# A two-layer decoder trunk on one core: attention's projections one step later, two of them held back, and longer delays in two chains

## The chip, the core and the metric

The kernel runs on one core of one Trainium2 chip, as one launch. The time is the device time of that core in microseconds. Every time below is from runs of the unchanged kernel or from the one execution that the profiler recorded.

## What is computed

Two layers on 256 tokens of width 1024, in fp32; layer 0 mixes tokens by a gated MLP, layer 1 by native sparse attention (NSA). Each layer also attends to 256 memory tokens, projects both results together, and ends with a SwiGLU feed-forward part.

```python
for i in range(2):
    h = rmsnorm(x, norm_mix[i])
    mem_n = rmsnorm(mem, norm_mem[i])
    mix, mem_q = gmlp_mixer(h, ...) if i == 0 else nsa_mixer(h, ...)
    mem_o = mem_cross_attention(mem_q, mem_n, w_mem_kv[i])    # 4 heads of 64
    x = x + concat([mix, mem_o]) @ w_out                      # 1024 -> 1024
    h = rmsnorm(x, norm_ffn[i])
    x = x + (silu(h @ wg) * (h @ wu)) @ wd                    # 1024 -> 2816 -> 1024
return rmsnorm(x, norm_final)
# gmlp_mixer: u, v = split(gelu(h @ w_in)); v = rmsnorm(v) * gain
#   mixed = per group g of 12: tril(w_s[g]) @ v[:, g] + b_s[g];  returns u * mixed
# nsa_mixer: 12 query heads, 4 key/value heads; compressed, selected and sliding
#   branches, each a softmax, summed with gates. k and v of the compressed branch:
#   silu(blocks @ w1) @ w2, 15 blocks of 32 tokens
```

## The kernel before

**Products.** Each fp32 operand is split into a high part H and a rest L, both fp32r, and each product is three matmuls into one PSUM bank: H by H, L by H, H by L (`mm3`, L228 to L230). `split` (L121) makes a pair: ACT copies the source to H (`wH`, `aH`, L122), then DVE subtracts H from the source (`wL`, `aL`, L123); `split_gained` (L127, L128) does it with a gain. So each weight tile of 128x1024 costs one ACT and one DVE pass, and waits for its DMA (`raw`, three buffers) and for one of seven slots for split weights; the slot comes free when the tile's last product has been made. Activations are split in the same way on their way from PSUM to SBUF. Two PSUM pools of four banks each are used: `mm` for sums that stay, `tr` for everything short-lived (transposes, scores, outputs of a head).

**Order.** The order of TensorE is the order in which the program is written (L90). Side chains (`v_chain`, `compress`, `mem_attention`, ...) are Python generators: `flow` keeps a running estimate of TensorE's time, adds to it at each product (`flow.tick`, L231), and resumes a chain when the time that it gave with `yield` is over. So `yield 3.0` says: put what follows on TensorE some 3 us of products later. ACT, DVE, POOL and the DMA queue are ordered by a scheduler, which takes the instruction of higher priority among those that are ready in its own plan; `tc.high_priority(offset=...)` lifts a stretch of code. `step` (L1015) runs its function with `HI = 150`. [...]

**Layer 0, the gate (L617 to L699).** `v_chain` transposes the masked w_s in three groups of four (L659, L660), ACT copies each to `wsT` (L661), `spatial(q)` makes four matmuls for each group (L639) and DVE adds the bias (L641); then four products `gm` of U and V (L671, DVE), each transposed (L674, line L244 of the helper) and split. Beside it TensorE does the projection of U (128x512 matmuls) and of the memory queries (128x256), whose result goes through L691 and L376 on DVE, and the memory keys and values (`mm<-mid,wH`).

**Layer 1, compression (L782 to L837).** The hidden layer of the compressed keys and values is summed in `ph` (L798), ACT applies Silu to its two halves (L808), and after a `yield` TensorE transposes it (L811, in the trace L244).

**Layer 1, attention (L1031 to L1072).** A step m of six handles one pair of heads. `scores(m)`: six matmul groups into four `tr` banks (L925, L927, L929); DVE adds the masks and finds the bounds (L945, L943); ACT takes the exponentials, eight of them (L949), and one for the compressed part (L961); DVE makes the scale `f` twice (L951, L952) and that of the compressed part, `smc` (L959 to L965); POOL multiplies the probabilities by `f` (L954), two passes each time. `turn(m)`: twelve transposes into three `tr` banks (L972, L978; L244), one more, `tc_`, into a fourth (L982), ACT copies them out (L974, L980, L983). `attend(m)`: 32 short matmuls into one `tr` bank `o` (L1001), then `split` (L1002): `aH` on ACT and `aL` on DVE. `mixed((m, tb))`: the output projection of that pair of heads for half tb of the tokens, six 128x512 matmuls (two `mm3`); it needs `aH` first and `aL` at its second matmul. The order at the end is

```python
step(scores, 4); mixed((0, 1)); step(attend, 2); step(turn, 3); mixed((2, 0))
step(scores, 5); mixed((1, 1)); step(attend, 3); step(turn, 4); mixed((3, 0))
step(attend, 4); step(turn, 5); mixed((4, 0), (2, 1)); step(attend, 5)
mixed((3, 1), (5, 0), (4, 1), (5, 1))
```

Of the kernel before, what the change touches and what calls it, by code (L numbers as in the profile page):

```python
# [26 lines left out]
class Flow:  # L27
# [10 lines left out]
    def _step(self):  # L38
        at, n, gen = heapq.heappop(self.heap)
        with self.tc.high_priority(offset=HI):  # L40
            try:
# [16 lines left out]


HI = 150  # L60
MEMLAT = 9.0
MEMCH = 0.0
VCH = 2.0
# [4 lines left out]
def body(tc, t, out):  # L68
    nc = tc.nc
    PE, ACT, DVE, POOL, SP = nc.tensor, nc.scalar, nc.vector, nc.gpsimd, nc.sync  # L70
    with ExitStack() as ctx:
# [49 lines left out]
        def split(H, L, src):  # L121
            ACT.copy(H, src)  # L122
            DVE.tensor_tensor(L, src, H.bitcast(F32), op=ALU.subtract)  # L123
# [118 lines left out]
        def transposes(ps, src, n, at=0):  # L242
            for j in range(n):
                PE.transpose(ps[:, (at + j) * 128 : (at + j + 1) * 128], src[:, j * 128 : (j + 1) * 128], ident)  # L244
            flow.now += n * 0.108

        def sumsq(src, acc, n):

            ACT.activation(junk[:, : src.shape[-1]], src, AF.Square, scale=n**-0.5, accum_out=acc)  # L249
# [17 lines left out]
        def blk(tb):  # L267
            return slice(tb * 128, (tb + 1) * 128)

        def kview(ps, n):  # L270
            return ps[:, : n * 128].rearrange("p (k n) -> p k n", k=n)
# [109 lines left out]
        def mem_attention(qTs, tb, kv, dst, done):  # L381
            qT = qTs[tb]

            scs = [tr(), tr()]
            for j in range(2):
                for i in range(2):
                    r = slice(i * 64, i * 64 + 64)
                    PE.matmul(scs[i][:, j * 256 : (j + 1) * 256], qT[r, j, :], kv[r, j, :], start=True, stop=True)  # L388
            flow.now += 1.1
            mx = tiny([128, 4], "mx")  # L390
            for i in range(2):
                DVE.reduce_max(mx[:, i * 2 : i * 2 + 2], scs[i].rearrange("p (j n) -> p j n", j=2), axis=AX.X)
            nb = tiny([128, 4], "nb")
            POOL.tensor_scalar(nb, mx, -SCALE, None, op0=ALU.mult)
            sm = tiny([128, 4], "sm")
            parts = [small([128, 2, 256]) for _ in range(2)]
            for i in range(2):
                for j in range(2):
                    n = i * 2 + j
                    ACT.activation(parts[i][:, j, :], scs[i][:, j * 256 : (j + 1) * 256], AF.Exp, bias=nb[:, n : n + 1],  # L400
                                   scale=SCALE, accum_out=sm[:, n : n + 1])
            rs = tiny([128, 4], "rs")
            DVE.reciprocal(rs, sm)
            for i in range(2):
                POOL.tensor_tensor(parts[i], parts[i], rs[:, i * 2 : i * 2 + 2].unsqueeze(2).to_broadcast([128, 2, 256]), op=ALU.mult)
            yield MEMLAT
            pTs = []
            for i in range(2):
                pt = tr()
                transposes(pt, parts[i].rearrange("p j n -> p (j n)"), 4)  # L410
                pT = small([128, 4, 128])
                ACT.copy(pT, kview(pt, 4))
                pTs.append(pT)
            yield 3.2
            o = tr()
            for j in range(2):
                for b in range(2):
                    for i in range(2):
                        h = (2 * j + i) * 64
                        PE.matmul(o[i * 64 : i * 64 + 64, blk(j)], kv[:, 2 + b, h : h + 64],  # L420
                                  pTs[i][:, j * 2 + b, :], start=b == 0, stop=b == 1)
            flow.now += 1.0
            split(dst[0][:, 6:8, blk(tb)], dst[1][:, 6:8, blk(tb)], kview(o, 2))
            done.append(1)
# [10 lines left out]
        def ffn(weights, nrm, after):  # L435
            accs = [[mm(), mm()], [mm(), mm()]]
            for ci, (nk, wg, wu, wd) in enumerate(weights):
# [4 lines left out]
                def gate(tb):  # L442
                    ps = tr()
                    gemm(ps, nrm.act, tb, wg, n)
                    sil[tb] = small([128, n])
                    with tc.high_priority(offset=HI):
                        ACT.activation(sil[tb], ps[:, :n], AF.Silu, scale=nrm.rstd[tb])
# [161 lines left out]
        def gelu(dst, ps, tb):  # L609
            with tc.high_priority(offset=HI):  # L610
                ACT.activation(dst, ps, AF.Gelu_apprx_tanh, scale=n0.rstd[tb])
# [36 lines left out]
        def v_chain():  # L648
            POOL.affine_select(wsr, wsr, pattern=[[0, 12], [-1, 128]], compare_op=ALU.is_ge, fill=0.0, base=0, channel_multiplier=1)
            for tb in range(2):  # L650
                ss = tiny([128, 2], "ss")
                sumsq(Vv[:, tb, 0:512], ss[:, 0:1], GW)
                sumsq(Vv[:, tb, 512:768], ss[:, 1:2], GW)
                r = rstd_of(ss)
                yield 1.5
                DVE.scalar_tensor_tensor(Vv[:, tb, :], Vv[:, tb, :], r, vg, op0=ALU.mult, op1=ALU.mult)
            yield 2.0
            for q in range(3):
                ps = tr()  # L659
                transposes(ps, wsr[:, q * 4 : q * 4 + 4, :].rearrange("p g s -> p (g s)"), 4)  # L660
                ACT.copy(wsT[:, q * 4 : q * 4 + 4, :], kview(ps, 4))  # L661
                yield 0.8
            for q in range(3):
                spatial(q)
                yield 1.0
            for c, n in ((0, 512), (512, 256)):
                for tb in range(2):
                    while tb not in u_done:
                        yield 0.3
                    gm = small([128, n])  # L670
                    DVE.tensor_tensor(gm, U[:, tb, c : c + n], Vv[:, tb, c : c + n], op=ALU.mult)  # L671
                    yield 1.0
                    ps = tr()
                    transposes(ps, gm, n // 128)  # L674
                    k = c // 128
                    split(mix[0][:, k : k + n // 128, blk(tb)], mix[1][:, k : k + n // 128, blk(tb)], kview(ps, n // 128))
            v_done.append(1)
# [8 lines left out]
        for tb in range(2):  # L686
            ps = mm()
            gemm(ps, n0.act, tb, WQ0, 256)
            mq = small([128, 256])
            with tc.high_priority(offset=HI):  # L690
                DVE.tensor_scalar(mq, ps[:, 0:256], n0.rstd[tb], None, op0=ALU.mult)  # L691
# [4 lines left out]
        for tb in range(2):  # L696
            flow.spawn(mem_attention(qT0, tb, kv0, mix, mo_done), 1.0 + 5.5 * tb)
# [34 lines left out]
        mix1 = acts()  # L732

        def rope(*a):
            with tc.high_priority(offset=HI):
                rope_(*a)
# [27 lines left out]
        def compress():  # L764
            X = [mqx[:, 512:1472].rearrange("p (a j n) -> p a j n", a=2, j=8),
                 mid([128, 2, 8, 60])]
            for s in range(2):
                for gp in range(2):
# [5 lines left out]
                    for part in range(2):  # L774
                        pe = gT[:, (PEV if s else PEK) + part * 8 : (PEV if s else PEK) + part * 8 + 8]
                        for par in range(2):
                            r = slice(par * 64, par * 64 + 64)
                            y = ps[r, :].rearrange("p (g c j a) -> p j g c a", g=2, j=8, a=2)[:, :, :, part : part + 15, par]
                            o = X[s][r, part, :, gp * 30 : gp * 30 + 30].rearrange("p j (g c) -> p j g c", g=2)
# [26 lines left out]
            POOL.memset(hS, 0.0)  # L806
            for s in range(2):
                ACT.activation(hS[s * 64 : s * 64 + 60, :], ph[s * 64 : s * 64 + 60, 0:256], AF.Silu)  # L808
            yield 3.0
            pt = tr()  # L810
            transposes(pt, hS, 2)  # L811
            hTk = small([128, 2, 60])
# [26 lines left out]
        for tb in range(2):  # L839
# [5 lines left out]
            v2 = small([128, 4, 2, 64])  # L845
            with tc.high_priority(offset=HI):
                ACT.activation(v2, twice(heads(ps[:, 256:512], 4)), AF.Copy, scale=n1.rstd[tb])
# [138 lines left out]
        def attend(m):  # L986
            pT0, pT1 = turned[m]
            o = tr()
            for tb in range(2):
                n = 3 if tb == 0 else 5  # L990
                for i in range(n):
                    for hh in range(2):
                        g = m // 3 + 2 * hh
                        c = slice(g * 64, g * 64 + 64)
                        if i == n - 1:
                            w, z = vc[:, tb, g, :], pcT[:, m % 2]
                        elif tb == 0:
                            w, z = V[:, i, 0, c], pT0[:, hh * 2 + i, :]
                        else:
                            w, z = V[:, i // 2, i % 2, c], pT1[hh][:, i, :]  # L1000
                        PE.matmul(o[hh * 64 : hh * 64 + 64, blk(tb)], w, z, start=i == 0, stop=i == n - 1)  # L1001
            split(mix1[0][:, m, :], mix1[1][:, m, :], o[:, 0:256])  # L1002

        soft, turned = {}, {}

# [7 lines left out]


        def step(f, *a):  # L1015
            with tc.high_priority(offset=HI):
                f(*a)

        ps = mm()
# [18 lines left out]
        def mixed(*parts):  # L1038
            for m, tb in parts:
                down(accs1, mix1, [m], [WO1[m]], m == 6, m == 5, after if m == 5 else None, (tb,))  # L1040
# [14 lines left out]
        step(turn, 2)  # L1055
        mixed((1, 0))
        step(scores, 4)
        mixed((0, 1))
        step(attend, 2)
        step(turn, 3)  # L1060
        mixed((2, 0))
        step(scores, 5)
        mixed((1, 1))
        step(attend, 3)
        step(turn, 4)
        mixed((3, 0))
        step(attend, 4)
        step(turn, 5)
        mixed((4, 0), (2, 1))
        step(attend, 5)  # L1070
        mixed((3, 1), (5, 0), (4, 1), (5, 1))
        flow.until(lambda: f1.rstd[0] is not None)  # L1072
# [65 lines left out]
```

## Time and profile before

| | us |
|---|---|
| median of 3 runs | 637.43 |
| lowest and highest | 636.39, 638.38 |
| the profiled execution | 638.98 |
| its span, first to last instruction | 637.3 |
| around the span (638.98 - 637.3) | 1.7 |
| TensorE busy in it | 618.8 (97%) |
| VectorE, ScalarE, GpSimd busy | 377.1, 327.0, 58.1 |

Busy times of different engines overlap, so they don't add up to the span. PE is TensorE, DVE VectorE, ACT ScalarE, POOL GpSimd. A row of a timeline gives an instruction's start and duration; on PE matmuls overlap (a 128x512 matmul lasts 0.39 us but the next starts 0.23 us after it), so lengths of work are best taken from one start to the next.

### The profile page before, as it was taken

Reading aid. Unit: us, or ns where it says so; the run is one execution under the profiler, and the core shown is the slowest. Engines: PE = TensorE matmul, PEld = TensorE weight load, DVE = VectorE, ACT = ScalarE, POOL = GpSimd, SP = SyncE. Lnnn points to the kernel's source line nnn. Section 1 sums busy time; section 2 is a strip of 40 time slices with the busy share of each in tenths; the row PEclk is TensorE's granted clock in tenths of the full one; section 3 lists DMA queues with packets and bytes.
Section 4 is the critical chain, followed back from the end, with each engine's and each line's share of the span. In section 5 each row is a group of like instructions: output and inputs, shape, how many; then the busy total and the mean of one; then the engine's idle time right before and its main releaser. Section 6 shows DMA issues by size and latency. Waiting matters only on the chain.

```text
span 637.3 us, 8843 instructions
## 1 busy us (share of the span) xinstructions
PE 618.8 (97%) x3382; PEld 512.1 (80%) x3382; DVE 377.1 (59%) x616; ACT 327.0 (51%) x553; POOL 58.1 (9%) x90
## 2 busy tenths in 40 slices
PE   8999999999999999999999999889999999999995
PEld 6879879888888888889876786668988888888884
DVE  4898457463645545476597489746644545546344
ACT  5785567443535344365544479746543535344333
POOL 0330111000000000002003106420000000000001
PEclk9999999999999999999999999989999999999998
DMA  7966254565555564744948552042554554636401
GB/s 239 374 225 230 74 190 141 198 202 192 162 188 182 172 224 136 260 132 121 354 140 273 123 134 61 8 145 87 198 181 150 205 191 162 234 134 231 163 0 66
DMA packets 57330, 109.69 MB, mean 172 GB/s; under 512 B 3428, under 2 KB 19400, under 8 KB 57288
## 3 DMA queue, kind: packets, MB, share of 16 engines
q1 hardware_dynamic: 57272, 109.12, 51.4%
q8 instruction: 26, 0.43, 0.3%
q14 instruction: 16, 0.13, 0.1%
q10 hardware_dynamic: 16, 0.00, 0.0%
HBM read 108.07 MB, written 1.05 MB: 171 GB/s over the span
## 4 chain that ended last, share of the span: by engine, by line
PE 84%; ACT 5%; DMA 4%; DVE 4%; issue 1%; POOL 1%; SPq 0%; POOLq 0%; ACTq 0%; DVEq 0%
PE tr L229 13%; PE mm L228 13%; PE mm L229 13%; PE tr L230 13%; PE tr L228 13%; PE mm L230 12%; PE tr L244 4%; ACT mid L949 3%; DMA wsr<-in_gmlp_w_s_dram 2%; DMA x<-in_x_dram 1%; PE tr L798 1%; DVE wL L123 1%; DMA raw<-in_w_mem_kv_dram 1%; DVE wL L128 1%; PE tr L388 1%
## 5 line engine op out<-in xcount | busy, mean ns | idle before, releaser
L123 DVE TENSOR_TENSOR wL<-raw,wH 128x1024 fp32r<-128x1024 f32 (+1 forms) x170 | 207.0, 1236 | 148.8 <-ACT wH L122 142.9
L122 ACT CAST wH<-raw 128x1024 fp32r<-128x1024 f32 (+1 forms) x170 | 173.8, 1043 | 150.3 <-PE tr L229 75.5
L228 PE MATMUL tr<-wH,aH 128*128 128x512 f32 (+1 forms) x384 | 143.8, 375 | 0.0
L229 PE MATMUL tr<-wH,aL 128*128 128x512 f32 (+1 forms) x384 | 142.8, 372 | 0.6 <-DVE aL L123 0.6
L230 PE MATMUL tr<-wL,aH 128*128 128x512 f32 (+1 forms) x384 | 142.7, 372 | 0.0
L228 PE MATMUL mm<-wH,aH 128*128 128x512 f32 (+2 forms) x224 | 87.4, 390 | 0.0
L229 PE MATMUL mm<-wH,aL 128*128 128x512 f32 (+2 forms) x224 | 83.4, 372 | 3.3 <-DVE aL L123 3.3
L230 PE MATMUL mm<-wL,aH 128*128 128x512 f32 (+2 forms) x224 | 83.3, 372 | 0.1
L229 PEld LDWEIGHTS tr<-wH,aL 128*128 128x128 f32 x384 | 72.4, 188 | 13.1 <-DVE aL L123 0.9
L230 PEld LDWEIGHTS tr<-wL,aH 128*128 128x128 f32 x384 | 72.3, 188 | 12.6
L228 PEld LDWEIGHTS tr<-wH,aH 128*128 128x128 f32 x384 | 72.3, 188 | 12.3
L228 PE MATMUL mm<-wH,mid 128*128 128x512 f32 (+1 forms) x208 | 79.2, 381 | 0.0
L229 PE MATMUL mm<-wH,mid 128*128 128x512 f32 (+1 forms) x208 | 77.9, 374 | 0.0
L230 PE MATMUL mm<-wL,mid 128*128 128x512 f32 (+1 forms) x208 | 77.8, 374 | 0.0
L228 PEld LDWEIGHTS mm<-wH,aH 128*128 128x128 f32 x224 | 42.6, 190 | 10.2 <-issue 4.5
L229 PEld LDWEIGHTS mm<-wH,aL 128*128 128x128 f32 x224 | 42.5, 190 | 9.8 <-DVE aL L123 4.2
L230 PEld LDWEIGHTS mm<-wL,aH 128*128 128x128 f32 x224 | 42.4, 189 | 7.8 <-DVE wL L128 0.5
L257 POOL TENSOR_SCALAR rstd<-ss 128x1 f32<-128x1 f32 x14 | 7.4, 526 | 435.4 <-ACT junk L249 431.2
L230 PEld LDWEIGHTS mm<-wL,mid 128*128 128x128 f32 x208 | 39.2, 188 | 7.1
L229 PEld LDWEIGHTS mm<-wH,mid 128*128 128x128 f32 x208 | 39.2, 189 | 6.9 <-DVE mid L123 0.5
L228 PEld LDWEIGHTS mm<-wH,mid 128*128 128x128 f32 x208 | 39.2, 188 | 6.7 <-ACT mid L122 0.4
L451 DVE SCALAR_TENSOR_TENSOR small<-tr,rstd,small 128x512 f32<-128x512 f32 (+1 forms) x24 | 16.9, 703 | 36.5 <-PE tr L230 36.5
(158 smaller groups left out, 649.9 us busy)
## 6 DMA issues: line engine op xcount, KB each, us to landing
raw<-in_ffn_w_down_dram SPq DMA_DIRECT2D x22, 1024.0 KB, 5.0
raw<-in_ffn_w_gate_dram SPq DMA_DIRECT2D x20, 1024.0 KB, 5.1
raw<-in_ffn_w_up_dram SPq DMA_DIRECT2D x20, 1024.0 KB, 5.1
raw<-in_nsa_w_in_dram SPq DMA_DIRECT2D x6, 1024.0 KB, 6.9
raw<-in_gmlp_w_in_dram SPq DMA_DIRECT2D x4, 1024.0 KB, 8.7
raw<-in_w_mem_kv_dram SPq DMA_DIRECT2D x4, 1024.0 KB, 5.8
raw<-in_gmlp_w_out_dram SPq DMA_DIRECT2D x4, 1024.0 KB, 6.7
raw<-in_nsa_w_out_dram SPq DMA_DIRECT2D x12, 256.0 KB, 5.0
```

The lines of the kernel that those rows point to most:

```text
L122: ACT.copy(H, src)
L123: DVE.tensor_tensor(L, src, H.bitcast(F32), op=ALU.subtract)
L128: DVE.scalar_tensor_tensor(L, src, g, H.bitcast(F32), op0=ALU.mult, op1=ALU.subtract)
L228: PE.matmul(ps, aH, bH, start=first, stop=False)
L229: PE.matmul(ps, aL, bH, start=False, stop=False)
L230: PE.matmul(ps, aH, bL, start=False, stop=last)
L244: PE.transpose(ps[:, (at + j) * 128 : (at + j + 1) * 128], src[:, j * 128 : (j + 1) * 128], ident)
L257: POOL.tensor_scalar(r, ss[:, 0:1], ss[:, 1:2], EPS, op0=ALU.add, op1=ALU.add)
L388: PE.matmul(scs[i][:, j * 256 : (j + 1) * 256], qT[r, j, :], kv[r, j, :], start=True, stop=True)
L451: DVE.scalar_tensor_tensor(h, ps[:, :n], nrm.rstd[tb], sil[tb], op0=ALU.mult, op1=ALU.mult)
L798: PE.matmul(ph[s * 64 : s * 64 + 60, 0:256], X[s][:, k // 8, k % 8, :], w1[q, s][:, j, :], start=k == 0, stop=k == 15)
L949: ACT.activation(o, o, AF.Exp, bias=nb[:, i : i + 1], scale=-1.0, accum_out=sm[:, i : i + 1])
```

## The change

A second priority `UP = 500` is added. The `turn` steps, the split at the end of `attend` and the copies of the memory attention's transposed probabilities get it. Three pieces of TensorE's order move: in layer 0 the first `spatial` comes 1.6 units of `flow` time later; the transposes of the compressed hidden layer come 3.0 later; and in the attention `mixed((0, 1))` goes from before `attend(2)` to behind `turn(3)`, `mixed((1, 1))` and `mixed((2, 1))` go one step later, and (4, 0) and (2, 1) swap. No instruction is added or removed, apart from lines that move by one or two numbers (L228 is L229 after the change, L952 is L954, L1001 is L1003). The orders of POOL and of the DMA queue are the same as before.

```diff
 HI = 150
+UP = 500
...
                 pT = small([128, 4, 128])
-                ACT.copy(pT, kview(pt, 4))
+                with tc.high_priority(offset=UP):
+                    ACT.copy(pT, kview(pt, 4))
...
                 ACT.copy(wsT[:, q * 4 : q * 4 + 4, :], kview(ps, 4))
-                yield 0.8
+                yield 0.8 if q < 2 else 2.4
...
                 ACT.activation(hS[s * 64 : s * 64 + 60, :], ph[s * 64 : s * 64 + 60, 0:256], AF.Silu)
-            yield 3.0
+            yield 6.0
...
-            split(mix1[0][:, m, :], mix1[1][:, m, :], o[:, 0:256])
+            with tc.high_priority(offset=UP):
+                split(mix1[0][:, m, :], mix1[1][:, m, :], o[:, 0:256])
...
         def step(f, *a):
-            with tc.high_priority(offset=HI):
+            with tc.high_priority(offset=UP if f is turn else HI):
                 f(*a)
...
         step(scores, 4)
-        mixed((0, 1))
         step(attend, 2)
         step(turn, 3)
+        mixed((0, 1))
+        step(scores, 5)
         mixed((2, 0))
-        step(scores, 5)
-        mixed((1, 1))
         step(attend, 3)
         step(turn, 4)
-        mixed((3, 0))
+        mixed((1, 1), (3, 0))
         step(attend, 4)
         step(turn, 5)
-        mixed((4, 0), (2, 1))
+        mixed((2, 1), (4, 0))
         step(attend, 5)
```

**TensorE at scores 4, before.** Rows from the last matmuls of `scores(4)` on; `mm` is the projection, `tr<-mid,V` attend 2, `tr<-ident,mid` turn 3.

```order
L929 MATMUL tr<-KT,QT 128x512 x2
L228 MATMUL mm<-wH,aH 128x512
L229 MATMUL mm<-wH,aL 128x512
L230 MATMUL mm<-wL,aH 128x512
L228 MATMUL mm<-wH,aH 128x512
L229 MATMUL mm<-wH,aL 128x512
L230 MATMUL mm<-wL,aH 128x512
L1001 MATMUL tr<-mid,V 64x128 x4
L1001 MATMUL tr<-pcx,vc 64x128 x2
L1001 MATMUL tr<-mid,V 64x128 x8
L1001 MATMUL tr<-pcx,vc 64x128 x2
L244 MATMUL tr<-ident,mid_3738 128x128 x2
```

The same place after the change:

```order
L931 MATMUL tr<-KT,QT 128x512 x2
L1003 MATMUL tr<-mid,V 64x128 x4
L1003 MATMUL tr<-pcx,vc 64x128 x2
L1003 MATMUL tr<-mid,V 64x128 x8
L1003 MATMUL tr<-pcx,vc 64x128 x2
L245 MATMUL tr<-ident,mid_3738 128x128 x2
L245 MATMUL tr<-ident,mid_3755 128x128 x2
L245 MATMUL tr<-ident,mid_3738 128x128 x4
L245 MATMUL tr<-ident,mid_3755 128x128 x4
L245 MATMUL tr<-ident,pcx 128x128
L229 MATMUL mm<-wH,aH 128x512
L230 MATMUL mm<-wH,aL 128x512
```

Attend 2 and turn 3 now follow scores 4 at once, and the projection that stood between them, (0, 1), comes behind the transpose of `pcx` (`tc_`).

**DVE behind the exponentials of scores 4, before.** `f4_3869` is the second scale, `smc_3875` the compressed part's, `wL_3936` a weight's rest, `aL_2651<-tr_3889` the rest of attend 2's output.

```order
L951 RECIPROCAL f4_3869<-sm4_3864 128x4
L962 TENSOR_REDUCE smc_3875<-pcx_3413 128x4
L952 TENSOR_TENSOR f4_3869<-f4_3869,gates_2751 128x4
L963 RECIPROCAL smc_3875<-smc_3875 128x4
L964 TENSOR_TENSOR smc_3875<-smc_3875,gatec_2752 128x4
L965 TENSOR_TENSOR pcx_3413<-pcx_3413,smc_3875 128x4x15
L123 TENSOR_TENSOR wL_3936<-raw_3422,wH_3935 128x1024
L123 TENSOR_TENSOR aL_2651<-tr_3889,aH_2650 128x256
```

The same place after the change:

```order
L953 RECIPROCAL f4_3869<-sm4_3864 128x4
L954 TENSOR_TENSOR f4_3869<-f4_3869,gates_2751 128x4
L124 TENSOR_TENSOR aL_2651<-tr_3883,aH_2650 128x256
L964 TENSOR_REDUCE smc_3875<-pcx_3413 128x4
L965 RECIPROCAL smc_3875<-smc_3875 128x4
L966 TENSOR_TENSOR smc_3875<-smc_3875,gatec_2752 128x4
L967 TENSOR_TENSOR pcx_3413<-pcx_3413,smc_3875 128x4x15
L124 TENSOR_TENSOR wL_3989<-raw_3422,wH_3988 128x1024
```

The output's rest `aL` moves ahead of the weight's rest and of the compressed part's four instructions; the weight's rest stays behind them and ahead of the masks of scores 5.

**DVE in layer 0, from the rest of the second memory weight to the first product `gm`, before** (`wL_543` to `wL_583` are memory weights, L641 the bias of a spatial group, L691 the scaled queries, L671 the product).

```order
L128 SCALAR_TENSOR_TENSOR wL_543<-raw_402,gT_107,wH_542 128x512
L641 TENSOR_TENSOR Vv_115<-tr_571,gT_107 128x4x2x64
L128 SCALAR_TENSOR_TENSOR wL_543<-raw_402,gT_107,wH_542 128x512
L128 SCALAR_TENSOR_TENSOR wL_561<-raw_402,gT_107,wH_560 128x512 x2
L641 TENSOR_TENSOR Vv_115<-tr_595,gT_107 128x4x2x64
L691 TENSOR_SCALAR small_619<-mm_578,rstd_243 128x256
L123 TENSOR_TENSOR wL_583<-raw_420,wH_582 128x1024
L671 TENSOR_TENSOR small_634<-U_114,Vv_115 128x512
```

The same place after the change:

```order
L129 SCALAR_TENSOR_TENSOR wL_543<-raw_402,gT_107,wH_542 128x512 x2
L129 SCALAR_TENSOR_TENSOR wL_561<-raw_402,gT_107,wH_560 128x512
L643 TENSOR_TENSOR Vv_115<-tr_589,gT_107 128x4x2x64
L129 SCALAR_TENSOR_TENSOR wL_561<-raw_402,gT_107,wH_560 128x512
L693 TENSOR_SCALAR small_613<-mm_572,rstd_243 128x256
L643 TENSOR_TENSOR Vv_115<-tr_607,gT_107 128x4x2x64
L124 TENSOR_TENSOR wL_577<-raw_420,wH_576 128x1024
L643 TENSOR_TENSOR Vv_115<-tr_628,gT_107 128x4x2x64
L124 TENSOR_TENSOR wL_643<-raw_420,wH_642 128x1024
L377 COPY small_637<-tr_634 128x256
L673 TENSOR_TENSOR small_654<-U_114,Vv_115 128x512
```

The first product now has three instructions more ahead of it: the third bias, a second 128x1024 weight's rest, and the copy of the queries. On TensorE twelve more matmuls of 128x256 stand ahead of its transposes than before.

## Rows read from the trace of the kernel before

**Rows 1.** The page: busy time, share of the span and instructions of each engine.

```profile
PE 618.8 (97%) x3382; PEld 512.1 (80%) x3382; DVE 377.1 (59%) x616; ACT 327.0 (51%) x553; POOL 58.1 (9%) x90
```

**Rows 2.** The waits of TensorE: who is waited for, us in total, times, the longest.

```profile
PE mm L229 <- DVE aL L123: 3.3, 2, 1.6
PE tr L244 <- DVE aL L123: 1.0, 1, 1.0
PE tr L244 <- issue: 0.8, 1, 0.8
```

**Rows 3.** Timeline of TensorE in the gate of layer 0: start, duration, instruction, and the idle time before it with what ended it.

```profile
45.89 0.40 PE L230 MATMUL mm<-wL,aH 128*128 128x512 f32 x1
47.21 1.16 PE L639 MATMUL tr<-Vv,wsT 128*128 128x128 f32 x8 [0.92 <-ACT wsT L661]
55.56 0.60 PE L244 MATMUL tr<-ident,small 128*128 128x128 f32 x4
```

**Rows 4.** Timeline of DVE there.

```profile
48.77 0.75 DVE L128 SCALAR_TENSOR_TENSOR wL<-raw,gT,wH 128x512 fp32r<-128x512 f32 x1 [1.01 <-ACT wH L127]
49.44 0.68 DVE L641 TENSOR_TENSOR Vv<-tr,gT 128x512 f32<-128x512 f32 x1
50.04 2.07 DVE L128 SCALAR_TENSOR_TENSOR wL<-raw,gT,wH 128x512 fp32r<-128x512 f32 x3
...
52.62 0.47 DVE L691 TENSOR_SCALAR small<-mm,rstd 128x256 f32<-128x256 f32 x1
53.02 1.21 DVE L123 TENSOR_TENSOR wL<-raw,wH 128x1024 fp32r<-128x1024 f32 x1
54.15 0.68 DVE L671 TENSOR_TENSOR small<-U,Vv 128x512 f32<-128x512 f32 x1
...
55.35 0.41 DVE L376 COPY small<-tr 128x256 f32<-128x256 f32 x1
```

**Rows 5.** Timeline of ACT there.

```profile
48.01 2.56 ACT L127 ACTIVATE wH<-raw,gT 128x512 fp32r<-128x512 f32 x4 [0.38 <-DMA raw<-in_w_mem_kv_dram]
```

**Rows 6.** Timeline of TensorE at the compressed hidden layer.

```profile
352.55 0.39 PE L230 MATMUL mm<-wL,aH 128*128 128x512 f32 x1
353.77 0.41 PE L244 MATMUL tr<-ident,small 128*128 128x128 f32 x2 [0.83 <-issue]
```

**Rows 7.** Timeline of ACT there.

```profile
353.29 0.38 ACT L808 ACTIVATE small<-tr 60x256 f32<-60x256 f32 x1
```

**Rows 8.** Timeline of TensorE at the end of the attention: turn 2's last transpose, scores 4, projection, attend 2, turn 3, its last transpose, projection; scores 5; turn 5, its last transpose, two projections, attend 5.

```profile
404.04 0.33 PE L244 MATMUL tr<-ident,pcx 128*128 128x128 f32 x1 [1.00 <-DVE aL L123]
...
405.69 0.73 PE L925 MATMUL tr<-KT,QT 64*128 64x271 f32 x4
...
407.43 0.50 PE L228 MATMUL mm<-wH,aH 128*128 128x512 f32 x1
...
409.01 0.66 PE L1001 MATMUL tr<-mid,V 128*64 128x128 f32 x8
...
410.91 1.53 PE L244 MATMUL tr<-ident,mid 128*128 128x128 f32 x12
412.51 0.33 PE L244 MATMUL tr<-ident,pcx 128*128 128x128 f32 x1
...
414.73 0.77 PE L229 MATMUL mm<-wH,aL 128*128 128x512 f32 x1 [1.65 <-DVE aL L123]
...
417.13 1.23 PE L925 MATMUL tr<-KT,QT 64*128 64x271 f32 x4
...
419.38 0.50 PE L228 MATMUL mm<-wH,aH 128*128 128x512 f32 x1
...
429.91 1.53 PE L244 MATMUL tr<-ident,mid 128*128 128x128 f32 x12
431.27 0.27 PE L244 MATMUL tr<-ident,pcx 128*128 128x128 f32 x1
...
434.25 0.66 PE L1001 MATMUL tr<-mid,V 128*64 128x128 f32 x8
```

**Rows 9.** Timeline of DVE there.

```profile
403.05 0.60 DVE L952 TENSOR_TENSOR f<-f,gates 128x4 f32<-128x4 f32 x1
403.57 0.41 DVE L123 TENSOR_TENSOR aL<-tr,aH 128x256 fp32r<-128x256 f32 x1
...
406.68 0.29 DVE L945 CUSTOM_DVE_ANT_0 mid<-tr,causal 128x128 f32<-128x128 f32 x1 [1.18 <-PE tr L927]
...
410.94 0.53 DVE L952 TENSOR_TENSOR f<-f,gates 128x4 f32<-128x4 f32 x1
...
412.26 2.08 DVE L123 TENSOR_TENSOR wL<-raw,wH 128x1024 fp32r<-128x1024 f32 x1
414.26 0.41 DVE L123 TENSOR_TENSOR aL<-tr,aH 128x256 fp32r<-128x256 f32 x1
```

**Rows 10.** Timeline of ACT there: a weight's high part.

```profile
410.69 1.03 ACT L122 CAST wH<-raw 128x1024 fp32r<-128x1024 f32 x1
```

**Rows 11.** Busy time by stretch: the stretch, us, busy time of PE, PEld, DVE, ACT and POOL with numbers of instructions, granted TensorE clock, DMA share, GB/s.

```profile
388.00:405.00 17.00, 14.59 (x134) 10.97 (x133) 15.26 (x67) 14.75 (x54) 9.60 (x12) 1.00 0.21 63
...
410.00:415.00 5.00, 3.28 (x33) 2.55 (x30) 3.93 (x8) 3.58 (x11) 3.07 (x4) 0.98 0.01 2
415.00:420.00 5.00, 5.00 (x20) 2.98 (x20) 1.34 (x10) 1.03 (x5) 0.00 (x0) 0.68 0.64 210
```

## The prediction, made before the change was run

> **What bounds the kernel.** I read the page first. TensorE is busy 618.8 us, 97% of the span, DVE 59%, ACT 51% [rows 1]. The change adds no matmul, so it can give back only idle time of TensorE, or time that TensorE loses by running slower. The list of TensorE's waits comes next: the largest entry is the second matmul of a projection waiting for `aL` from DVE, 3.3 us in two waits; then a transpose that waits 1.0 for `aL` and one that waits 0.8 [rows 2]. The timelines tell where these lie: in the attention's end at 404 and 414.73 us [rows 8], at 353.77 in the compression [rows 6], and 0.92 at 47.21 in the gate [rows 3]. These are the three places where the change reorders TensorE. [...]
>
> **Part A, the gate.** TensorE could have gone on at about 46.12 (0.23 after its last start) and goes on at 47.21: 1.09 lost, start to start [rows 3]. The later `spatial` puts twelve 128x256 matmuls there, about 0.12 each, 1.43 in all, and the wait closes. But these twelve are now missing, and three DVE instructions are new, ahead of the first `gm` transpose, which runs at 55.56 now [rows 3]. TensorE would be there at 55.56 - 1.09 + 1.43 = 55.9. DVE can't start its list before 48.77, because ACT's split behind it waits for a memory weight's DMA [rows 4, 5], which no order moves. From 48.77, by starts in [rows 4]: four rests of 128x512 at 0.66 (2.65), three biases at 0.60 (1.80), the scaled queries 0.40, two weights' rests at 1.13 (2.26), the copy of the queries 0.33, together 7.44, so the product runs from 56.21 to 56.89. TensorE waits 1.0 there for what it gained before. Net gain 0.1; the bounds are 0 less a small loss of 0.3 (if the transposes' banks come late too) and 0.9 (if DVE gets through sooner).
>
> **Part B, the compression.** TensorE's last matmul starts at 352.55, the transposes at 353.77, which is 0.99 more than the 0.23 of a matmul [rows 6]. They wait for ACT's second Silu, at its end at 353.67 [rows 7]. With 3.0 us more of products between, two more `mm3` and the memory attention's outputs run first and the Silu is over two us early. Gain 1.0. What comes next is the copy of the transposed hidden layer on DVE, for which the same products keep the cover; I hold at 1.0, and 0.8 is the low end. The earlier copies of the memory attention cost nothing: they swap with one copy on ACT, whose reader is farther off.
>
> **Part C, the end of the attention.** Lengths of work from start to start [rows 8]: scores 1.74 (405.69 to 407.43), one projection half 1.58 (to 409.01), attend 1.90 (to 410.91), twelve transposes 1.53, the same in the last step, where the banks are free, 1.36 (429.91 to 431.27), `tc_` with one half 1.65 (404.04 to 405.69), `tc_` with two halves 2.98 (431.27 to 434.25). Now the stretch from 405.69 to 434.25 takes 28.56. In it lie the two waits for `aL`, because on DVE the rest `aL` stands behind a weight's rest that lasts 2.08 [rows 9], and the slow clock: 412.51 to 417.13 is 4.62 where 1.65 of work and 1.65 of wait make 3.30, and scores 5 takes 2.25 (to 419.38) instead of 1.74, so 1.32 + 0.51 = 1.83.
>
> After the change `aL` goes ahead of that weight, and attend 2 follows scores 4 at once, so the exponentials of scores 4 become the hurdle. By the new order: scores 4 from 405.69, attend 2 from 407.43, turn 3 from 409.33 to 410.86. Its `tc_` takes the bank that attend 2's output leaves, so it waits for `aL`. DVE comes to that behind the second `f`, which starts at 410.94 [rows 9]; it lasts 0.53 there. The row at 403.05 (0.60) has the order on DVE that is the new one everywhere: 0.52 from `f` to `aL`, 0.47 from `aL` to `tc_` [rows 8, 9]. So `tc_` at 411.93, wait 1.0 (403.05's twin waited 1.00 as well). Then `tc_` and (0, 1) to 413.58, scores 5 to 415.32, (2, 0) to 416.90, attend 3 to 418.80, turn 4 to 420.33. The weight's rest is now ahead of the masks of scores 5 on DVE, and its slot comes free with (0, 1): 1.03 on ACT [rows 10] from about 413.4, then 1.21 on DVE [rows 4], to 415.65. The masks, which would start 0.99 behind scores 5 (406.68 against 405.69 [rows 8, 9]) at 414.57, start 1.1 later. `tc_` of turn 4 follows 5.25 behind them, as 411.93 behind 406.68: 420.9, a wait of 0.6. Then 2.98 to 423.9, attend 4 to 425.8, turn 5 1.36 to 427.1, two halves to 430.1, where attend 5 starts at 434.25 now. Gain **4.2** (434.25 - 430.1), of which 1.83 is the clock and 2.4 the rest. The moved projections need no new data: their weights were split for the other half of the tokens, which runs earlier, and the `mm` banks stay theirs. What is held back ends before attend 5, as now.
>
> **Sum.** Against the profiled execution: 638.98 - 0.1 - 1.0 - 4.2 = 633.7. That execution is 1.55 above the median, near one loss of 1.83, so I take it that the middle run lacks the slow stretch: 637.43 - 0.1 - 1.0 - 2.4 = 633.9. I forecast **633.8**.
>
> The clock hangs on more than the row of one stretch. The rows show that the stretch from 388 to 405 has the new order already (in the code scores 2 and 3 are followed by attend and turn at once), with a wait of 1.00 at its end [rows 8], and there it was granted 1.00 throughout [rows 11]; it fell behind a wait of 1.65, which the new order doesn't have. [...]
>
> **Rivals.**
> - The gate pays in full: DVE reaches `gm` a us sooner than I lay it out, 633.8 - 0.8 = 633.0. Against it: the instructions of DVE's list from 48.77 on stand end to end, only its start could move.
> - The wait comes back at `tc_`: attends 2 and 3 get their `aL` 1.0 and more later than laid out (POOL holds `f` longer, or the weight's rest is in its 2.08 form ahead of scores 5), and the two waits stay at 1.65 or so. Then the 2.4 are gone and A and B remain: 637.43 - 1.1 = 636.3. For it: a rest of the same shape takes 2.08 in [rows 9] and 1.21 in [rows 4], and which of the two it will be near 414.5 no row tells.
> - One fall of the clock somewhere in 405 to 430, as now: 633.8 + 1.8 = 635.6; two: 637.5.
> - The other side: the clock falls at turn 3's `tc_` and stays low until the projections are through. Five matmuls at the low level take 2.40 (414.73 to 417.13), 0.48 each, against 1.58 / 6 = 0.26 [rows 8]: 0.22 for each of the 36 matmuls of the six halves, 7.9, and 0.5 for scores 5: 642.2. It is slower than before from about 25 matmuls at that level ((639.3 - 633.8) / 0.22). [...]
>
> **How the numbers follow.** A measurement here can tell 0.3%, 1.9 us: faster is below 635.5, slower above 639.3. Chances: forecast 0.64, the gate in full 0.07, the wait back at `tc_` 0.13, one or two falls of the clock 0.11, clock stays low 0.05. Faster: 0.64 + 0.07 and a part of one fall 0.03 = 0.74; slower 0.05; the rest 0.21 is no change. The range goes below to the gate in full (637.43 - 0.9 - 1.0 - 2.4 = 633.1) and 1.0 more, as far as the runs shown lie from their median, 632.1, and above just past the wait at `tc_`, 636.5.
>
> **What would show it.** In the profile after: no wait at L641 (0.92 now), but one of about 1.0 at the four transposes of `gm` near 56; no gap at the transposes of the compressed hidden layer; in the waits, `mm L230 <- aL` gone and `tr L245 <- aL` at 0.9 to 1.0 (turn 3) and 0.4 to 0.6 (turn 4), with `aL` 0.5 behind the second `f`; granted clock 1.00 from 405 to 430; scores 4 to attend 5 24.4 us long instead of 28.56. The prediction is wrong if the clock falls without a wait above 1.0, if the masks of scores 5 start over 1.5 late, or if the stretch gains and the time does not, because the feed-forward part behind it then waits for its weights.

## The result

The changed kernel takes 632.95 us (632.81 to 634.55, 4 runs) beside 637.12 of the kernel before on the same chip: ratio 0.9937, 95% interval 0.9924 to 0.995, so 4.2 us less with 3.2 to 4.8 inside the interval. It was forecast at 633.8, in a range of 632.1 to 636.5. Its profiled execution took 634.55, span 632.8. Beside later runs the changed kernel took 632.88 against 636.93, ratio 0.9946 (0.9932 to 0.9959). Here and below the ratio is not the quotient of the two medians; where the two say different things, both are given.

The waits of TensorE in the profile after, as in [rows 2]: who is waited for, us in total, times, the longest.

```profile
PE tr L245 <- DVE aL L124: 2.5, 3, 1.0
...
PE tr L230 <- DVE aL L124: 0.6, 1, 0.6
PE tr L245 <- ACT mid L976: 0.6, 1, 0.6
PE tr L927 <- ACT mid L976: 0.5, 1, 0.5
PE tr L245 <- issue: 0.3, 1, 0.3
...
PE tr L245 <- DVE small L673: 0.2, 1, 0.2
```

The 3.3 us at the second matmul of a projection are gone, and the wait for `aL` at a transpose has grown from one to three. The entries for `wsT` and for the hidden layer of the compression are gone too; 0.2 for a `gm` product (L673) and 0.3 at another transpose are new.

TensorE at the end of the attention, after: the row of scores 4, attend 2, turn 3 with its last transpose, scores 5, turn 4 with its last transpose, and attend 5, as in [rows 8].

```profile
405.59 0.73 PE L927 MATMUL tr<-KT,QT 64*128 64x271 f32 x4
...
407.34 0.66 PE L1003 MATMUL tr<-mid,V 128*64 128x128 f32 x8
...
409.24 1.53 PE L245 MATMUL tr<-ident,mid 128*128 128x128 f32 x12
411.77 0.33 PE L245 MATMUL tr<-ident,pcx 128*128 128x128 f32 x1 [1.00 <-DVE aL L124]
...
413.42 0.73 PE L927 MATMUL tr<-KT,QT 64*128 64x271 f32 x4
...
418.63 1.53 PE L245 MATMUL tr<-ident,mid 128*128 128x128 f32 x12
420.63 0.33 PE L245 MATMUL tr<-ident,pcx 128*128 128x128 f32 x1 [0.48 <-DVE aL L124]
...
429.88 0.66 PE L1003 MATMUL tr<-mid,V 128*64 128x128 f32 x8
```

From scores 4 to attend 5 it is 24.29 us, where [rows 8] have 28.56. Each stop lies 0.2 to 0.3 before the one laid out in the prediction (411.93, 413.58, 420.9, 430.1), of which 0.10 was there at the start. DVE in the same stretch, as in [rows 9]: the second scale `f`, the output's rest behind it, the weight's rest, the first mask of scores 5.

```profile
410.78 0.59 DVE L954 TENSOR_TENSOR f<-f,gates 128x4 f32<-128x4 f32 x1
411.30 0.41 DVE L124 TENSOR_TENSOR aL<-tr,aH 128x256 fp32r<-128x256 f32 x1
...
414.37 1.23 DVE L124 TENSOR_TENSOR wL<-raw,wH 128x1024 fp32r<-128x1024 f32 x1 [1.13 <-ACT wH L123]
415.51 0.28 DVE L947 CUSTOM_DVE_ANT_0 mid<-tr,causal 128x128 f32<-128x128 f32 x1
```

`aL` stands 0.52 behind `f`, as at 403.05 in [rows 9]; the weight's rest comes after it, in its form of 1.2 us, and the masks start when it ends.

The clock by stretch, after: us, busy time of PE, PEld, DVE, ACT, POOL, granted clock, DMA share, GB/s, as in [rows 11].

```profile
405.00:410.00 5.00, 5.00 (x54) 3.61 (x54) 3.56 (x23) 3.08 (x15) 0.61 (x2) 1.00 0.01 3
410.00:415.00 5.00, 4.00 (x27) 2.55 (x24) 3.16 (x8) 3.58 (x10) 2.97 (x4) 1.00 0.01 2
415.00:420.00 5.00, 5.00 (x52) 4.07 (x50) 4.08 (x26) 4.16 (x19) 1.52 (x2) 1.00 0.57 210
420.00:430.00 10.00, 9.52 (x74) 7.63 (x74) 4.19 (x8) 5.67 (x11) 1.77 (x3) 1.00 0.48 159
```

### The profile page after: what moved, and what is told of

The parts are those of the page before. It is cut to its first block, busy times and chain, and to the rows that moved or that the text cites. A ratio compares the mean times of both kernels' runs of the same rounds, so it can differ in the third digit from the quotient of the medians.

```text
span 632.8 us, 8848 instructions
## 1 busy us (share of the span) xinstructions
PE 618.1 (98%) x3382; PEld 513.9 (81%) x3382; DVE 377.1 (60%) x616; ACT 327.3 (52%) x553; POOL 58.2 (9%) x90
## 4 chain that ended last, share of the span: by engine, by line
PE 90%; ACT 5%; DVE 2%; DMA 1%; issue 1%; POOL 0%; SPq 0%; POOLq 0%; ACTq 0%; DVEq 0%
PE mm L229 14%; PE mm L230 14%; PE mm L231 14%; PE tr L230 13%; PE tr L231 13%; PE tr L229 13%; PE tr L245 5%; ACT mid L951 3%; PE tr L800 1%; DMA x<-in_x_dram 1%; PE tr L389 1%; PE tr L422 1%; PE tr L1003 1%; ACT wH L123 1%; DVE wL L124 0%
## 5 line engine op out<-in xcount | busy, mean ns | idle before, releaser
L229 PE MATMUL tr<-wH,aH 128*128 128x512 f32 (+1 forms) x384 | 143.8, 375 | 0.0
L229 PE MATMUL mm<-wH,aH 128*128 128x512 f32 (+2 forms) x224 | 87.7, 391 | 0.0
L229 PEld LDWEIGHTS tr<-wH,aH 128*128 128x128 f32 x384 | 72.3, 188 | 12.3
L229 PE MATMUL mm<-wH,mid 128*128 128x512 f32 (+1 forms) x208 | 79.2, 381 | 0.0
L229 PEld LDWEIGHTS mm<-wH,aH 128*128 128x128 f32 x224 | 42.9, 191 | 9.6 <-issue 4.0
L229 PEld LDWEIGHTS mm<-wH,mid 128*128 128x128 f32 x208 | 39.2, 189 | 6.7 <-ACT mid L123 0.4
```

The lines of the kernel that those rows point to most:

```text
L229: PE.matmul(ps, aH, bH, start=first, stop=False)
```

## The experiments

Three lengths are taken from each profile, start to start on TensorE: the **gate** from the 140th to the 260th matmul into an `mm` bank (counted from 0), the **compression** from the 920th to the 960th, the **attention** from scores 4 to attend 5. Outside them every run agrees within 0.1 us (277.5 us from the gate to the compression, 39.7 from there to scores 4, 203.0 from attend 5 to the end), apart from two runs told of below, so they hold the whole difference, apart from the start: the 140th matmul starts at 44.2 to 46.4 in different runs. No change here touches that. TensorE waits there for x (1.7 us before, 1.4 after), and in the profile after its 128x512 matmuls start 0.43 us apart up to 10.54 and 0.23 apart from 12.60 on; in the one before they are 0.23 apart from 11.10 on already.

| run | ratio (95%) | gate | compression | attention |
|---|---|---|---|---|
| before (profile above) | 1 | 20.53 | 22.71 | 28.56 |
| before again | one run | 19.69 | 23.00 | 27.01 |
| changed | 0.9937 (0.9924 to 0.995) | 19.60 | 22.31 | 24.29 |
| changed again | 0.9946 (0.9932 to 0.9959) | 20.00 | 21.95 | 24.27 |
| attention only | 0.9946 (0.9927 to 0.9965) | 20.82 | 23.02 | 24.28 |
| yields only | 0.9984 (0.9972 to 0.9996) | 20.82 | 21.97 | 26.99 |
| order without the priority | 0.9929 (0.991 to 0.9948) | 19.60 | 21.97 | 24.28 |
| priority without the order | 0.9985 (0.997 to 0.9999) | 19.84 | 22.03 | 26.99 |
| `tc_` behind a projection | 0.9915 (0.9897 to 0.9932) | 19.76 | 22.51 | 23.03 |

**Which part carries it.** The changed kernel with both yields as before (attention only), and the kernel before with both yields as changed (yields only); the diff is the first one's:

```diff
-                yield 0.8 if q < 2 else 2.4
+                yield 0.8
...
-            yield 6.0
+            yield 3.0
```

> The attention's order and the priorities as changed, both yields as before. Theory 1 (the attention carries nearly all; the gate is worth about 0.2 and the compression 0.4, as the two traces put it): 4.2 less 0.6, so 3.6 us under the kernel before, ratio about 0.994; the wait of 0.9 at the first spatial matmul and the gap of 0.8 ahead of the hidden layer's transposes are back, and the stretch from scores 4 to attend 5 is 24.3 us. Theory 2 (the gate and the compression pay their waits in full, 2.1 by starts): 2.1 under, ratio 0.9967.

> Only the two longer yields, attention and priorities as before. Theory 1: 0.6 us under the kernel before (ratio 0.999), with a new wait of about 1.0 at the first gm transposes, less by what the start of the kernel is late. Theory 2: 2.1 under (ratio 0.9967).

Measured: 634.56 and 636.59 against 637.09, so 2.5 and 0.5 us less by the medians, 3.4 (2.2 to 4.7) and 1.0 (0.3 to 1.8) by the ratios. The times alone do not part the theories; the traces do, and theory 1 holds. With the attention only, the stretch takes 24.28 and both waits are back (0.8 for `wsT`, 0.8 at the hidden layer). With the yields only, the gate has a wait of 1.4 in place of the 0.9 (below), and the gain is the compression's, 22.7 to 22.0.

**The priority.** The changed kernel with all priorities as before (the split and the probabilities' copies too), and the priorities without the moved projections; the diff is the first one's:

```diff
-UP = 500
+UP = 150
...
-            with tc.high_priority(offset=UP if f is turn else HI):
+            with tc.high_priority(offset=HI):
```

> The changed kernel with every priority as before (150; none on the probabilities' copies). Theory 1 (the new order of TensorE alone puts aL ahead of the weight's rest): as the changed kernel, 4.2 us under the kernel before, ratio 0.9935, waits of 1.0 and 0.5 at the last transposes of turns 3 and 4. Theory 3 (the priority 500 carries it): the two 1.65 waits return and only the 0.6 of the yields is left, ratio 0.999.

> The priorities and both yields as changed, the projections at the places of before. Theory 1: aL stays behind the weight's rest on DVE, both waits of 1.65 stay, 0.6 us under the kernel before, ratio 0.999. Theory 3: the waits go without the new order, 2.5 to 4.2 under, ratio 0.996 to 0.9935.

633.56 (the interval overlaps that of the changed kernel) and 636.49, the time of the yields alone. Theory 3 falls. With the priority alone TensorE still waits as before:

```profile
PE mm L230 <- DVE aL L124: 3.3, 2, 1.6
```

and DVE still has the weight's rest ahead of `aL`, in its long form:

```profile
410.99 2.08 DVE L124 TENSOR_TENSOR wL<-raw,wH 128x1024 fp32r<-128x1024 f32 x1
412.99 0.41 DVE L124 TENSOR_TENSOR aL<-tr,aH 128x256 fp32r<-128x256 f32 x1
```

What puts `aL` first is the moved projections; no run moves one of them alone, and the trace points to (0, 1). That weight's slot comes free with (0, 1): before, ahead of attend 2, so that ACT splits the weight at 410.69 and the output's `aH` behind it [rows 10]; with the priority alone it is the same, the weight at 409.42 and `aH` at 410.35. After, behind turn 3, so that ACT gets to it later:

```profile
413.29 1.05 ACT L123 CAST wH<-raw 128x1024 fp32r<-128x1024 f32 x1 [0.75 <-PE mm L230]
```

**What holds the attention now.** The last transpose of turns 3 and 4 is taken out of `turn` into a function of its own, `turn_c`, and issued behind a half that needs nothing of it:

```diff
+        LATE = (3, 4)
...
         mixed((0, 1))
+        turn_c(3)
...
-        mixed((1, 1), (3, 0))
+        mixed((1, 1))
+        turn_c(4)
+        mixed((3, 0))
```

> The changed kernel with the last transpose of turns 3 and 4 moved behind a projection half that needs nothing of it: turn 3's behind (0, 1), turn 4's between (1, 1) and (3, 0). Theory 1 (the 1.0 and 0.5 that are left at that transpose are the wait for aL, with nothing else late behind it): both waits go, scores 4 to attend 5 takes 22.8 instead of 24.28 us, time 1.5 under the changed kernel, ratio to the kernel before about 0.991. Theory 4 (the exponentials of the next step are late as well, so the wait moves on to the attend or the turn behind it): 24 us or more, ratio 0.9935.

Measured 632.13 us, ratio 0.9915 (0.9897 to 0.9932), attention 23.03: the two waits go and 1.25 us with them, nearly the 1.5 of theory 1. Its median is the lowest of this study. That it is faster than the changed kernel its trace shows, by 1.25 us; the intervals of the two times overlap. Turn 2 treated alike, with every half of the second token block one step earlier:

```diff
         step(turn, 2)
+        mixed((0, 1))
+        turn_c(2)
         mixed((1, 0))
...
-        mixed((2, 1), (4, 0))
+        mixed((3, 1), (4, 0))
         step(attend, 5)
-        mixed((3, 1), (5, 0), (4, 1), (5, 1))
+        mixed((4, 1), (5, 0), (5, 1))
```

> As the run before, with turn 2 treated alike: (0, 1) ahead of its last transpose, (1, 1) ahead of turn 3's, (2, 1) ahead of turn 4's, (3, 1) and (4, 0) behind turn 5, (4, 1), (5, 0), (5, 1) at the end. Theory 1: three waits go (1.0, 1.0, 0.5), scores 0 to attend 5 takes 49.8 instead of 52.26 us, time 2.5 under the changed kernel, ratio about 0.9895. Theory 4: 51 us or more, the waits come back at the attends.

635.23, ratio 0.9969 (0.9956 to 0.9982): slower than the changed kernel. Scores 0 to attend 5 takes 51.2 us, with one half more in it than in the changed kernel (about 1.5, which the expectation forgot): 49.7 for the same work, as in theory 1. The loss is at a place that neither theory had: from attend 5 to the end it takes 206.9 us with one half less to do, where all other runs take 203.0. Only one half now stands behind (5, 0) where there were two, so the norm of the first tokens is late for the feed-forward part; the run after this one, with the end as changed, does not have the loss. TensorE's timeline and the clock there:

```profile
433.27 1.30 PE L245 MATMUL tr<-ident,x 128*128 128x128 f32 x8
436.98 0.58 PE L229 MATMUL tr<-wH,aH 128*128 128x256 f32 x1 [2.41 <-ACT aH L123]
```

```profile
435.00:440.00 5.00, 2.55 (x10) 2.25 (x11) 3.86 (x7) 2.42 (x6) 3.28 (x4) 0.68 0.54 199
440.00:445.00 5.00, 5.00 (x30) 5.00 (x30) 2.39 (x4) 1.69 (x3) 0.00 (x0) 0.64 0.00 0
```

So turn 2 got a half from the other side instead, (7, 1), which stood ahead of turn 0, and the end stayed as changed:

```diff
-        mixed((6, 1), (7, 1))
+        mixed((6, 1))
...
         step(turn, 2)
+        mixed((7, 1))
+        turn_c(2)
         mixed((1, 0))
```

> The run with the last transposes of turns 3 and 4 behind a projection, and turn 2's too: half (7, 1) is held back for it from its place between scores 1 and turn 0; the order at the end of the attention stays that of the changed kernel. Theory 1: turn 2's wait of 1.0 goes and nothing else moves, 2.2 us under the changed kernel, ratio to the kernel before about 0.990. Theory 4 (turn 0, now 1.5 us sooner behind scores 1, waits for the probabilities or a bank): the 1.0 comes back ahead of turn 0 or of scores 2, time as with turns 3 and 4 alone, about 1.2 under.

> The changed kernel once more, beside the run above and on the same chip. All theories: 3.5 to 4.2 us under the kernel before, ratio 0.9935 to 0.9945; scores 4 to attend 5 24.3 us at full clock. The gate's length is 19.6 to 20.8 by how early the memory weight lands against TensorE.

636.80 and 632.88 against 636.93: the first is back at the time of before, worse than theory 4 had it. Turn 1 is now too early for POOL and DVE:

```profile
392.09 0.87 PE L245 MATMUL tr<-ident,mid 128*128 128x128 f32 x6 [0.52 <-POOL mid L956]
394.66 0.66 PE L245 MATMUL tr<-ident,mid 128*128 128x128 f32 x4 [1.69 <-POOL mid L956]
397.22 0.45 PE L245 MATMUL tr<-ident,pcx 128*128 128x128 f32 x1 [1.91 <-DVE pcx L967]
```

and the granted clock, 1.00 from 390 to 395, is 0.57 over the five us from 395. At the 0.50 that the fall in the kernel before has, that puts the start of this one at about 395.7, in the last of these waits (an estimate from the 0.57):

```profile
395.00:400.00 5.00, 3.09 (x10) 2.00 (x8) 1.03 (x8) 1.15 (x4) 1.17 (x2) 0.57 0.00 0
```

From scores 0 to scores 4 this run takes 33.24 us where the others take 28.0. The half that stood behind scores 1 was the cover of POOL's and DVE's work, not spare.

**The gate.** One product was put on POOL:

```diff
-                    DVE.tensor_tensor(gm, U[:, tb, c : c + n], Vv[:, tb, c : c + n], op=ALU.mult)
+                    eng = POOL if c == 0 and tb == 0 else DVE
+                    eng.tensor_tensor(gm, U[:, tb, c : c + n], Vv[:, tb, c : c + n], op=ALU.mult)
```

> The changed kernel with the first product of U and V (256 tokens' first half, 512 columns) on POOL instead of DVE. Theory 1 (the gate is now held by DVE's list, which starts with the landing of a memory weight): the wait at the first gm transposes goes and the gate from its 140th to its 260th product takes 19.6 us also when the weight lands late, where it took 20.8; 0 to 1.2 under the changed kernel, by how the start falls. Rival: POOL's product of 128x512 lasts so long that the wait stays, 20.5 or more, no gain.

632.80, ratio 0.9924 (0.9905 to 0.9943); the gate takes 20.94, so the wait has not gone, but not for the rival's reason:

```profile
52.98 2.16 POOL L674 TENSOR_TENSOR small<-U,Vv 128x512 f32<-128x512 f32 x1 [11.37 <-DVE Vv L643]
```

The product is there at 55.14. What waits instead, 1.15 from 55.85 on, are the transposes behind it, those of the queries of the second tokens, which come through DVE's list at 56.48 as well:

```profile
54.49 1.73 DVE L124 TENSOR_TENSOR wL<-raw,wH 128x1024 fp32r<-128x1024 f32 x1
56.15 0.41 DVE L377 COPY small<-tr 128x256 f32<-128x256 f32 x1
56.48 0.47 DVE L694 TENSOR_SCALAR small<-mm,rstd 128x256 f32<-128x256 f32 x1
```

So it is the whole list of DVE that is late, not the product. Taking the product (0.68) off it hardly made it shorter, since the weight's rest beside POOL's product took 1.73 instead of the 1.21 of [rows 4].

**The clock.** The kernel before once more:

> The kernel before once more, for its clock and its gate. Theory 5 (the fall of the clock at 414.78 was chance, since two runs had the same waits of 1.65 at full clock): granted clock 1.00 through scores 4 to attend 5, and 27.0 us for that stretch instead of 28.56. Theory 6 (the first wait of 1.65 brings it in this kernel): a fall again, 28.5 us.

636.78 us. The same two waits of 1.65, clock 1.00 throughout, attention 27.01: theory 5. Here are the two stretches with the waits in that run:

```profile
410.00:415.00 5.00, 3.26 (x24) 2.40 (x21) 3.94 (x8) 2.95 (x7) 2.43 (x3) 1.00 0.10 14
...
420.00:425.00 5.00, 3.28 (x30) 2.51 (x27) 3.94 (x8) 3.35 (x9) 2.83 (x4) 1.00 0.32 105
```

With the yields alone and with the priority alone it is the same. So of four profiles with these waits one shows a fall.

The mean granted clock of each execution says how often it falls. It is 0.994 in the profiled execution with the fall, and 0.996 to 0.999 in the nine profiles that have none before their last 5 us. Of 55 executions of the kernel before, taken beside these runs, 20 have 0.995 or less, with a median of 638.07 us, and 35 have more, with 636.49: 1.58 apart, as much as the attention with the fall is longer than without (28.56 - 26.99 = 1.57). With the yields alone it is 1 of 12, with the priority alone 6 of 12, and of 33 executions with the changed attention (five kernels) none. The mean does not tell where the clock fell, but the fall is no rarity in the kernel before, and it comes with the old order of the attention.

## Why the prediction was right, step by step

**The attention** was laid out rightly, and the size of its gain was between the two that the prediction gave. At full clock the stretch goes from 27.0 to 24.3: 2.7, where 2.4 stood in the sum from the median and 4.2 in that from the profiled execution. The 0.3 that lack are in the clock term: the fall cost 1.57, and the prediction took 1.83, so it left too little for the rest. The stretch from `tc_` of turn 3 to scores 5 takes 3.57 at full clock (before again), where the prediction had 1.65 + 1.65 = 3.30: a wait listed as 1.65 costs 1.92 from start to start. The places of the new waits (1.0 and 0.5 at `tc_` of turns 3 and 4) and the late masks are as forecast, and moving `tc_` shows that these waits are what is left there. That `aL` goes first because of the moved projections, not the priority, the prediction did not say; two runs show it.

The short form of the weight's rest was taken from [rows 4], and the prediction said that no row tells which form it will be. POOL's rows do, by its products with `f`. Before, they run to 413.26 and so beside the first 1.0 us of the rest at 412.26; after, they end at 413.16, and the rest starts at 414.37:

```profile
411.65 1.61 POOL L954 TENSOR_TENSOR mid<-mid,f 128x256 f32<-128x256 f32 x2 [0.19 <-DVE smc L963]
```

```profile
411.55 1.61 POOL L956 TENSOR_TENSOR mid<-mid,f 128x256 f32<-128x256 f32 x2 [0.18 <-ACT mid L976]
```

So the late rest gains twice: it is out of the way of `aL`, and it is out of POOL's. The rest takes 2.08 in the profile before (412.26), in before again (411.62) and with the priority alone (410.99), and 1.23 in the one after.

**The compression** was forecast at 1.0 and gave 0.7, below the 0.8 of its low end. The gap of 0.83 is gone in all profiles with the longer yield. Some runs, the profiled one among them, lose 0.3 at another transpose three us earlier (`issue`, 0.3 in the waits after), with the yield as without it, so it is not the yield's, and like must be compared with like: without that loss 22.71 against 21.95 to 22.03, with it 23.00 and 23.02 against 22.31 and 22.51.

**The gate** was forecast at 0.1, with one wait in place of the other, and the single runs seem to say otherwise: 20.53 before, 19.60 after. But the length follows how late ACT starts on the second memory weight, with which DVE's list starts. From the start of the 140th matmul to that start on ACT it is 2.81 us before (48.01 - 45.20, [rows 5] and the same matmul's start) and 1.33 after. Over the runs, length less this lateness is 17.72, 17.70 and 17.87 with the short yield (lateness 2.81, 3.12, 1.82) and 17.64, 17.65, 17.65 and 17.67 with the long one (3.18, 2.19, 2.11, 2.33); below a lateness of 1.7 the length is 19.60. So at the same lateness the long yield is worth 0.05 to 0.2. DVE with the yields alone, at a lateness of 3.18, and the wait that TensorE has there:

```profile
48.84 2.08 DVE L128 SCALAR_TENSOR_TENSOR wL<-raw,gT,wH 128x512 fp32r<-128x512 f32 x3 [1.22 <-ACT wH L127]
```

```profile
PE tr L244 <- DVE small L671: 1.4, 1, 1.4
```

In the profiled execution of the change TensorE came 1.2 us later into the gate than before, after a late start, so only 0.2 of that wait is seen. The product on POOL, with a lateness of 3.48, takes 20.94, 0.2 under this line. In five of the seven profiles ACT's start ends a wait of 0.3 to 0.8 us for the landing; in before again and changed again ACT comes to it straight from its own list, which had waited for the first memory weight. That ACT's start, and by it the landing, sets the length rests on the line of these seven profiles; no run moved the load, so it is not shown by an experiment.

**The sum.** 2.7 + 0.7 + 0.1 = 3.5 at full clock, as the prediction's 2.4 + 1.0 + 0.1; that the two sums are equal is luck, 0.3 too little in the attention against 0.3 too much in the compression. The executions of before without the fall have a median of 636.49, 3.5 and 3.6 above the 632.95 and 632.88 of the changed kernel. The 4.2 and 4.05 between the medians of all executions hold falls as well; the ratios give 4.0 (3.2 to 4.8) and 3.4 (2.6 to 4.3). The forecast was 0.85 too high by the time it started from: it took the middle run, 637.43, as one without the slow stretch. The clock of that run is not on record; it took 0.9 more than the 636.49.

**The rivals.** The wait for `aL` did come to `tc_`, but at the 1.0 and 0.5 laid out. The gate did not pay in full. The clock stayed at 1.00 through 405 to 430 in all six profiles with the changed attention, with scores, attend and turn back to back, so neither a fall nor a clock that stays low came. The row from 388 to 405 in [rows 11], with the same order at 1.00, had spoken against both.

## What to carry to other kernels

Where one engine's list is fixed, look at what frees the buffers of the instruction that is in the way: moving the product that frees a weight's slot behind the critical result kept a pass of 2.08 us out of its way, while a higher priority for the result changed nothing by itself: ACT still took the weight first. Held-back work is a cover that can be given out once: two of three further moves took the cover from a place that needed it and lost more than they gained. And a part whose length follows a DMA's landing must be compared at the same landing, or one pair of profiles credits a change with the difference between two starts. In the same way a median over executions of which a third (20 of 55 here) have a mean granted clock of 0.995 or less is no time at full clock, and a forecast that starts from it is off by a part of the fall.

## What the runs showed of the hardware

The clock's fall is not told by the length of a wait alone: of four profiles with the same two waits of 1.65 us one has a fall, right behind the first of them (3.4 us at a granted clock of 0.50, 1.57 us lost). It also fell at the wait of 2.41 (0.68 over 435 to 440, 0.64 over 440 to 445), and at the last of three waits (0.52, 1.69, 1.91) within 6 us (0.57 over 395 to 400, 0.87 over 400 to 410); at a level of 0.50 these means come to 6.8 and 6.9 us, an estimate. In these two kernels 12 of 12 and 10 of 11 executions have a mean clock of 0.995 or less.

A weight's rest on DVE was longer in most cases beside a two-operand product on POOL: in the profiles before and after, the 320 rests of 128x1024 that met no such product took 1.21 to 1.23 us, and 10 of the 12 that met one took 1.50 to 2.08. A 128x512 fp32 product of two SBUF operands took 2.16 us on POOL, once and beside two such rests, and 0.68 on DVE; POOL's products of that size with `f` took 1.04.
